# Six raw weight buffers for four, four common buffers fewer, and two steps moved in a block of a split-precision SwiGLU

## The chip, the cores and the metric

The kernel runs on one core of one Trainium2 chip. The metric is the device time in microseconds (us) of one execution; the median of several runs is compared. TensorE (PE) multiplies, VectorE (DVE) and ScalarE (ACT) work on its operands and results, GpSimd (POOL) does a few small things, and SyncE (SP) issues nearly all weight loads.

## The reference, cut to what matters

One decoder layer on 256 tokens of width 2048, in float32: a half-step SwiGLU FFN, a token mixer (sparse attention beside a recurrent branch), and a second FFN.

```python
D_MODEL, SEQ, D_FF = 2048, 256, 5632
def swiglu(h, w_in, w_out):
    a, b = jnp.split(h @ w_in, 2, axis=-1)
    return (jax.nn.silu(a) * b) @ w_out

h = layer_norm(DN_ALPHA * h + 0.5 * swiglu(h, ffn1_w_in, ffn1_w_out), ln1_g, ln1_b)
...
merged = g_attn * (y_attn @ w_attn_branch) + g_rnn * (y_rnn @ w_rnn_branch)
h = layer_norm(DN_ALPHA * h + merged @ w_out, ln2_g, ln2_b)
h = layer_norm(DN_ALPHA * h + 0.5 * swiglu(h, ffn2_w_in, ffn2_w_out), ln3_g, ln3_b)
```

## The kernel before

**Split operands.** Every float32 operand is kept as two parts, high (`wh`, `xs`/`hs`, `gh`) and low (`wl`, ..., `gl`), and a product is three matmuls: high x high, high x low, low x high (lines 734, 735, 736). A weight piece is 128 x 1024 numbers (512 KB). SP loads it (lines 192 and 206) into a raw buffer; ACT rounds it to `wh` (line 300); DVE subtracts that to get `wl` (line 301). High and low halves live in five buffers each (`HL_BUFS`), so piece n is split when piece n - 5 has been multiplied. `unit` asks for loads 8 pieces ahead and splits 4 ahead.

**Buffers.** `raw` tiles (4 KB a partition, `RAW_BUFS` = 4) hold loaded pieces. `u` tiles (2 KB a partition, `U_BUFS` = 53) are the common pool: activations in halves, sums of activations, residual, gate results, rows of gains and biases, attention's and the recurrent branch's tiles, and in the mixer the four quarters of a "quad" piece (loaded at line 204). Pieces P1 and Q5 of the FFN have buffers of their own (`k0`, four, and `k1`, three).

**An FFN** has 11 blocks of 512 hidden columns for gate and up. In blocks 1 to 10 most of the input product is done in Strassen's way with 7 products for 8: for each of three chunks (four k-tiles each) there are pieces P1, Q5, P6, Q3, P2, P7, Q4, each 6 matmuls, where some weights are sums of others, made by DVE in place (line 222): P6 needs P1 + Q5's quarter and the loaded P6 quarter, Q4 needs P1's buffer and the loaded P2 quarter. The fourth chunk is plain (`c`, four pieces of 12 matmuls). The output product of the block before is interleaved (`o`, 8 pieces of 12 matmuls).

**Banks and the join.** A block has four sums in PSUM: B and D in banks `bp`, A and E in the two banks `mm`. B starts with P1 and D with Q5. When P1 is complete, ACT writes A = -B (line 819 through `urgent`); P6 and then P7 add to A; after P7 ACT writes E = -A. D's first part is copied to `zd` when Q5 is complete, A's first part to `zu` when P6 is. The block's last plain piece completes all four; then comes the **join** (lines 853 to 863): silu of B and E on ACT, and on DVE zu += D, zu *= silu(B), zd += A, zd *= silu(E). Only zd += A reads bank A for the last time, so the next block's A can be written only after it. Both results are transposed on TensorE (line 1209) and split to `gh` and `gl` for the output product. An output pair of banks `ob` is copied out and the next pair seeded by ACT (lines 1238 and 1226).

**What sets the order.** PE, SP and POOL run in the order in which the code is written, which for an FFN is the plan of `wide_plan`: `STEADY` for blocks 2 to 9, `LAST` for block 10, a list of its own for block 1. In the strings, `o`, `c` and the form names are pieces in order, and `h` takes the next of the following block's head (P1, Q5, P1, Q5, P1, Q5), whose pieces stand among the present block's. ACT and DVE are ordered by a scheduler, which prefers what is marked urgent among what it holds for ready.

Of the kernel before, what the change touches and what calls it, by code (L numbers as in the profile page):

```python
# [12 lines left out]
OP = mybir.AluOpType  # L13
# [32 lines left out]
for _k, _w in (("ln1_g", NK), ("ln1_b", NK), ("ln2_g", NK), ("ln2_b", NK), ("ln3_g", 4), ("ln3_b", 4), ("conv_w", 4 * NR),  # L46
# [4 lines left out]

LAG = 2

U_BUFS = 53
T_BUFS = 8
RAW_BUFS = 4
K0_BUFS = 4
K1_BUFS = 3
HL_BUFS = 5
# [11 lines left out]
WGA, WAB, WRB, WO = (), (0, 1, 2, 3,), (0, 1, 2, 3,), (0, 1, 2,)  # L71


STEADY = ("o P6 o Q3 P6 Q3 o P6 o Q3 P2 o P7 o P7 P7 "
          "P2 P2 c Q4 o Q4 h c Q4 h o h c h h h c")
LAST = "o o P6 Q3 P6 Q3 o o P6 Q3 P2 P7 P7 P7 P2 P2 c Q4 Q4 c Q4 c c o o"


def wide_plan():

    def fast(n):
        return FAST[:2] if n == 1 else FAST

    def group(n, *items):
        return [(n, f, fast(n)[i]) for f, i in items if i < len(fast(n))]

    def head(n):  # L90
        return group(n, ("P1", 0), ("Q5", 0), ("P1", 1), ("Q5", 1), ("P1", 2), ("Q5", 2)) if n < NBK else []

    plan = [(0, "c", k) for k in range(NK)]
    for n in range(1, NBK):
        fill = [(n, "o", 0)]
        h = head(n + 1)
        plain = [(n, "c", k) for k in range(NK) if k // 4 not in fast(n)]
        if n == 1:
            plan += group(n, ("P1", 0), ("P1", 1), ("Q5", 0), ("Q5", 1), ("P6", 0), ("Q3", 0), ("P6", 1), ("Q3", 1))
            plan += 2 * fill + group(n, ("P2", 0)) + 2 * fill + group(n, ("P7", 0), ("P7", 1)) + 2 * fill  # L100
            plan += group(n, ("P2", 1))
            c0, c1, c2, c3 = (plain[i::4] for i in range(4))
            plan += c0 + group(n, ("Q4", 0), ("Q4", 1)) + h[:1] + c1 + h[1:3] + c2 + h[3:] + c3
            continue
        left = {}
        for f in (LAST if n == NBK - 1 else STEADY).split():
            i = left[f] = left.get(f, -1) + 1
            plan += fill if f == "o" else plain[i:i + 1] if f == "c" else h[i:i + 1] if f == "h" else group(n, (f, i))
    return plan


# [33 lines left out]
class Weights:  # L145
# [33 lines left out]
    def load_to(self, i):  # L179
        nc = self.nc  # L180
        while self.loaded <= min(i, len(self.pieces) - 1):
            ap, form = self.pieces[self.loaded]
            k = self.key(self.loaded)
            if isinstance(form, tuple):
                if form[0] in QUARTERS:
# [4 lines left out]
                    else:  # L190
                        t = self.pool.tile([P, PIECE], F32, name=f"raw{self.loaded}", tag="raw", bufs=RAW_BUFS)
                    nc.sync.dma_start(t, ap)
                    self.quarter[form[1], j] = t
            elif k not in self.raw:
# [5 lines left out]
                else:  # L200
                    t = self.pool.tile([P, PIECE], F32, name=f"raw{self.loaded}", tag="raw", bufs=RAW_BUFS)
                if form in QUADS.values():
# [52 lines left out]
    def small(self, name):  # L255
        return self.pool.tile([P, 512], F32, name=name, tag="u", bufs=U_BUFS)

# [119 lines left out]
def tile_layer(ctx, tc, x_fm, x_tm, pos, f1a, f1o, wA, wki, wB, wG, lru, lru_x, wab, wrb, wo, f2a, f2o,  # L377
# [5 lines left out]
    V, A, T, G = nc.vector, nc.scalar, nc.tensor, nc.gpsimd  # L383
    count = [0]

    def name(s):
        count[0] += 1
        return f"{s}{count[0]}"

    def U(s="u", dt=F32):  # L390
        return pool.tile([P, 512], dt, name=name(s), tag="u", bufs=U_BUFS)

# [28 lines left out]
    def BP():  # L421
        return psum.tile([P, 512], F32, name=name("bp"), tag="bp", bufs=4)
# [49 lines left out]
    for i in range(NR + LAG):  # L472
# [4 lines left out]
        if i >= LAG:  # L477
            g, c = divmod(i - LAG, TPG)
# [253 lines left out]
    def three(ps, xh, xl, w, start, stop, seeded=False):  # L732
        h, l = (v.rearrange("p (a h c) -> p a c h", h=2, c=P) for v in w)
        T.matmul(ps, xh, h, start=start, stop=False, skip_group_check=seeded)  # L734
        T.matmul(ps, xh, l, start=False, stop=False, skip_group_check=seeded)  # L735
        T.matmul(ps, xl, h, start=False, stop=stop, skip_group_check=seeded)  # L736

    def tokens(ps, x, t, w, start, stop, seeded=False):
        h, l = x(t) if callable(x) else (x[:, i, t * P:(t + 1) * P] for i in range(2))
        three(ps, h, l, w, start, stop, seeded)  # L740
# [67 lines left out]
    def xop(x, q, i, t):  # L808
        def op(r):
            v = x[4 * q + 2 * r + i]  # L810
            return v[:, 0, t * P:(t + 1) * P], v[:, 1, t * P:(t + 1) * P]
        return op

    def sop(forms, q, i):
        return lambda r: tuple(v[:, i * P:(i + 1) * P] for v in forms[2 * q + r])

    def urgent(f, *args, **kw):
        with tc.high_priority():
            f(*args, **kw)  # L819

    def blocksW(x, forms, fill, done):

        last = {(n, f): i for i, (n, f, k) in enumerate(PLAN)}
        bank = {n: {} for n in range(NBK)}
        z = {n: {} for n in range(NBK)}  # L830
        c = [None, None]

        def banks(t):
            if not c[t]:
                c[t] = [(CB, OB)[t]() for _ in range(2)]
            return c[t]

        def first(k, end):
            ws = [W.unit(512) for _ in range(2)]
            for t in range(2):  # L840
                for j in range(2):
                    tokens(banks(t)[j], x[k], t, ws[j], k == 0, k == NK - 1)
            for t in range(2 if end else 0):
                s = U("z")
                urgent(A.activation, s, c[t][0], AF.Silu)
                urgent(V.tensor_tensor, s, s, c[t][1], op=OP.mult)
                done(0, t, s)

        def plain(n, k, end):
            ws = [W.unit(512) for _ in range(2)]  # L850
            for t, j, b in ((0, 0, "B"), (0, 1, "D"), (1, 1, "A"), (1, 0, "E")):
                tokens(bank[n][b], x[k], t, ws[j], False, end, True)
            if end:
                v, ps = z[n], bank[n]
                s = [U("zs"), U("zs")]
                urgent(A.activation, s[0], ps["B"], AF.Silu)
                urgent(A.activation, s[1], ps["E"], AF.Silu)
                urgent(V.tensor_tensor, v["u"], ps["D"], v["u"], op=OP.add)
                urgent(V.tensor_tensor, v["u"], v["u"], s[0], op=OP.mult)
                done(n, 0, v["u"])  # L860
                urgent(V.tensor_tensor, v["d"], ps["A"], v["d"], op=OP.add)
                urgent(V.tensor_tensor, v["d"], v["d"], s[1], op=OP.mult)
                done(n, 1, v["d"])
                del bank[n], z[n]

        def product(n, form, k, end):
            b, op = {"P1": ("B", xop(x, k, 0, 0)), "P2": ("B", xop(x, k, 1, 0)), "Q3": ("D", sop(forms, k, 3)),
                     "Q4": ("E", xop(x, k, 1, 1)), "Q5": ("D", sop(forms, k, 0)), "P6": ("A", sop(forms, k, 1)),
                     "P7": ("A", sop(forms, k, 2))}[form]
            ps = bank[n]  # L870
            new = b not in ps
            if new:
                ps[b] = BP()
            for r in range(2):
                three(ps[b], *op(r), W.unit(512), new and r == 0, end and r == 1, form not in ("P1", "Q5"))
            if not end:
                return
            if form == "P1":
                ps["A"] = CB()
                urgent(A.activation, ps["A"], ps["B"], AF.Copy, scale=-1.0)  # L880
            elif form == "Q5":
                z[n]["d"] = U("zd")
                urgent(A.activation, z[n]["d"], ps["D"], AF.Copy)
            elif form == "P6":
                z[n]["u"] = U("zu")
                urgent(A.activation, z[n]["u"], ps["A"], AF.Copy)
            elif form == "P7":
                ps["E"] = CB()
                urgent(A.activation, ps["E"], ps["A"], AF.Copy, scale=-1.0)

        skip = 0
        if getattr(x, "halves", None):
            eager(x, banks)
            skip = 4
        for i, (n, form, k) in enumerate(PLAN):
            end = i == last[n, form]
            if i < skip:
                continue
            if form == "o":
                fill()  # L900
            elif n == 0:
                first(k, end)
            elif form == "c":
                plain(n, k, end)
            else:
                product(n, form, k, end)
# [384 lines left out]
    qT, kT, v, qiT = [None] * 8, [None] * 2, [None] * 2, [None] * 4  # L1291
# [182 lines left out]
    for b in a_order:  # L1474
# [9 lines left out]
        ps = blockA(hs)  # L1484
        if b == 5:
            for t in range(2):
                h, l = U("v", F32R), U("v", F32R)
# [13 lines left out]
    for nb in range(4):  # L1501
        if WGA and nb == WGA[0]:
            forms = make_forms(hs, QG)
        ps = column_block(hs, forms, MIXED["wG"].get(nb))
# [6 lines left out]
    for nb in range(4):  # L1511
        ps = column_block(ya, forms, MIXED["wab"].get(nb))
# [91 lines left out]
    for j in range(NR + LAG):  # L1604
# [5 lines left out]
        if j < NR:  # L1610
            ps = blockB(hs)
# [15 lines left out]
            ps = blockB(hs)  # L1627
# [3 lines left out]
        if j >= LAG:  # L1631
            i = j - LAG
            g, c = divmod(i, TPG)
# [5 lines left out]
            if c == TPG - 1:  # L1639
                ps = BP()  # L1640
# [31 lines left out]
    for nb in range(4):  # L1672
        if WO and nb == 3:
            mforms = make_forms(mg, U)
        ps = column_block(yr, forms, MIXED["wrb"].get(nb))
        for t in range(2):
            d = gr[nb][t]
# [115 lines left out]
```

## Time and profile before

| | us |
|---|---|
| median of 3 runs | 2253.88 |
| lowest and highest | 2251.0, 2257.98 |
| profiled execution | 2250.04 |
| its span (first to last instruction) | 2248.2 |

In the profile a row names the line, the engine, the operation and the tiles without their numbers, and ends with the idle time before it and what ended that. PEld is the weight load of TensorE, which runs beside the matmuls. Matmuls are pipelined and their ends are modelled: they overlap in the rows, so that a stall is seen from start to start. The first FFN lies between about 0 and 680 us, the mixer up to 1560, the second FFN behind it.

### The profile page before, as it was taken

How to read it: one execution, taken by the hardware profiler on the slowest of the kernel's cores; microseconds unless marked ns; L12 is line 12 of the kernel's file. 1: busy time of each engine (PE TensorE's matmuls, PEld its weight loads, DVE VectorE, ACT ScalarE, POOL GpSimd, SP SyncE). 2: the span in 40 equal slices, each digit the busy share in tenths (PEclk: the TensorE clock that was granted, in tenths of full speed). 3: DMA queues.
4: the chain of work that ended last, by engine and by line, in shares of the span. 5: the costliest groups of instructions: out<-in, count | busy, mean ns of one | idle time of the engine just before them, and what ended most of it. 6: DMA issues, size and time to landing. Idle time of an engine off the chain costs nothing.

```text
span 2248.2 us, 30930 instructions
## 1 busy us (share of the span) xinstructions
PE 2219.8 (99%) x11164; PEld 1939.3 (86%) x11164; DVE 1958.7 (87%) x2617; ACT 1559.6 (69%) x2222; POOL 22.4 (1%) x58
## 2 busy tenths in 40 slices
PE   9999999999999999999999999999999999999999
PEld 8888888888888888889999888898888888888887
DVE  7899999999988887678788886898999999999997
ACT  6777777777766556555688885555777777777774
POOL 0000000000001000000000000000000000000000
PEclk9999999999999999999999999999999999999999
DMA  8666655566666555566655566556666656665664
GB/s 302 215 225 218 205 192 203 197 204 215 211 206 219 175 182 164 161 214 199 209 177 188 184 203 235 194 194 195 215 220 210 219 199 223 220 209 193 206 213 157
DMA packets 133498, 459.33 MB, mean 204 GB/s; under 512 B 15040, under 2 KB 17856, under 8 KB 133344
## 3 DMA queue, kind: packets, MB, share of 16 engines
q1 hardware_dynamic: 130608, 449.37, 59.9%
q0 software_dynamic: 2160, 6.94, 1.0%
q8 instruction: 87, 1.43, 0.3%
q10 hardware_dynamic: 576, 1.05, 0.1%
q14 instruction: 67, 0.55, 0.1%
HBM read 455.20 MB, written 2.10 MB: 203 GB/s over the span
## 4 chain that ended last, share of the span: by engine, by line
PE 62%; DVE 17%; DMA 8%; issue 7%; ACT 5%; POOL 0%; ACTq 0%; SPq 0%; DVEq 0%; POOLq 0%
DVE wl L301 11%; PE ob L735 8%; PE ob L736 7%; PE ob L734 7%; PE mm L734 7%; PE mm L735 7%; PE mm L736 7%; DVE k L222 4%; DMA raw<-f2a 4%; DMA raw<-f1a 4%; PE bp L736 3%; PE bp L734 3%; PE bp L735 3%; ACT wh L300 3%; PE ob L723 2%
## 5 line engine op out<-in xcount | busy, mean ns | idle before, releaser
L301 DVE TENSOR_TENSOR wl<-raw,wh 128x1024 fp32r<-128x1024 f32 (+2 forms) x734 | 858.2, 1184 | 137.6 <-ACT wh L300 132.6
L300 ACT ACTIVATE wh<-raw 128x1024 fp32r<-128x1024 f32 (+2 forms) x734 | 741.4, 1025 | 320.0 <-PE mm L736 127.1
L301 DVE TENSOR_TENSOR wl<-k,wh 128x1024 fp32r<-128x1024 f32 x290 | 349.3, 1220 | 37.3 <-ACT wh L300 35.3
L300 ACT ACTIVATE wh<-k 128x1024 fp32r<-128x1024 f32 x290 | 302.7, 1056 | 112.4 <-DVE k L222 55.0
L735 PE MATMUL ob<-wl,gh 128*128 128x512 f32 x640 | 244.4, 382 | 9.8 <-DVE wl L301 9.8
L734 PE MATMUL ob<-wh,gh 128*128 128x512 f32 x640 | 244.6, 382 | 1.4 <-ACT ob L1226 1.4
L736 PE MATMUL ob<-wh,gl 128*128 128x512 f32 x640 | 242.7, 379 | 0.0
L222 DVE TENSOR_TENSOR k<-k,raw 128x1024 f32<-128x1024 f32 x174 | 211.6, 1219 | 32.0 <-DMA raw<-f1a 16.5
L734 PE MATMUL mm<-wh,hs 128*128 128x512 f32 x418 | 161.6, 387 | 0.0
L736 PE MATMUL mm<-wh,hs 128*128 128x512 f32 x418 | 158.5, 379 | 0.4 <-DVE hs L1054 0.4
L735 PE MATMUL mm<-wl,hs 128*128 128x512 f32 x418 | 158.5, 379 | 0.2 <-DVE wl L301 0.2
L735 PEld LDWEIGHTS ob<-wl,gh 128*128 128x128 f32 x640 | 121.0, 189 | 33.0 <-DVE wl L301 17.0
L734 PEld LDWEIGHTS ob<-wh,gh 128*128 128x128 f32 x640 | 121.0, 189 | 19.2 <-ACT ob L1226 2.8
L736 PEld LDWEIGHTS ob<-wh,gl 128*128 128x128 f32 x640 | 121.0, 189 | 17.1 <-DVE gl L819 0.5
L1238 ACT ACTIVATE y<-ob 128x512 f32<-128x512 f32 x152 | 89.5, 590 | 65.8 <-PE ob L736 65.7
L734 PE MATMUL ob<-wh,hs 128*128 128x512 f32 x304 | 118.4, 390 | 1.0 <-ACT hs L1053 1.0
L736 PE MATMUL ob<-wh,hs 128*128 128x512 f32 x304 | 115.5, 380 | 0.6 <-DVE hs L1054 0.6
L735 PE MATMUL ob<-wl,hs 128*128 128x512 f32 x304 | 115.2, 379 | 0.0
L723 PE MATMUL ob<-hs,wh 128*128 128x512 f32 x336 | 111.2, 382 | 0.0
L734 PE MATMUL bp<-wh,sh 128*128 128x512 f32 (+1 forms) x298 | 107.8, 362 | 1.3 <-ACT zd L819 1.3
L723 PE MATMUL mm<-hs,wh 128*128 128x512 f32 x320 | 106.7, 384 | 0.0
L735 PE MATMUL bp<-wl,sh 128*128 128x512 f32 (+1 forms) x298 | 106.1, 356 | 0.0
(404 smaller groups left out, 4828.2 us busy)
## 6 DMA issues: line engine op xcount, KB each, us to landing
raw<-f2a SPq DMA_DIRECT2D x118, 512.0 KB, 4.3
raw<-f1a SPq DMA_DIRECT2D x116, 512.0 KB, 4.5
raw<-f1o SPq DMA_DIRECT2D x88, 512.0 KB, 4.2
raw<-f2o SPq DMA_DIRECT2D x88, 512.0 KB, 3.7
raw<-wB SPq DMA_DIRECT2D x80, 512.0 KB, 4.5
raw<-wA SPq DMA_DIRECT2D x64, 512.0 KB, 3.5
raw<-wG SPq DMA_DIRECT2D x64, 512.0 KB, 3.6
k<-f1a SPq DMA_DIRECT2D x58, 512.0 KB, 6.9
```

The source lines that it names most:

```text
L222: self.nc.vector.tensor_tensor(v, v, self.quarter[q, j], op=OP.add)
L300: nc.scalar.activation(hp, src, AF.Copy)
L301: self.last = nc.vector.tensor_tensor(lp, src, hp, op=OP.subtract)
L723: T.matmul(ps, w[0], turns(x.rearrange("p a t -> p (a t)")), start=first, stop=False)
L734: T.matmul(ps, xh, h, start=start, stop=False, skip_group_check=seeded)
L735: T.matmul(ps, xh, l, start=False, stop=False, skip_group_check=seeded)
L736: T.matmul(ps, xl, h, start=False, stop=stop, skip_group_check=seeded)
L1238: A.activation(Y[t][nb], open_ps[t], AF.Copy, scale=0.5)
```

## The change

Four edits:

- `RAW_BUFS` goes from 4 to 6 and `U_BUFS` from 53 to 49: the same bytes, moved from the common pool to raw pieces, for the whole kernel.
- The last Q5 piece of the following block (the sixth of its head) no longer stands ahead of the block's last plain piece but behind the first output piece of the next block (`H`), in `STEADY`, `LAST` and the list of block 1.
- In the join the urgent instruction zd += A is written ahead of zu += D.

```diff
-U_BUFS = 53
+U_BUFS = 49
-RAW_BUFS = 4
+RAW_BUFS = 6
...
-STEADY = ("o P6 o Q3 P6 Q3 o P6 o Q3 P2 o P7 o P7 P7 "
-          "P2 P2 c Q4 o Q4 h c Q4 h o h c h h h c")
-LAST = "o o P6 Q3 P6 Q3 o o P6 Q3 P2 P7 P7 P7 P2 P2 c Q4 Q4 c Q4 c c o o"
+STEADY = ("o H P6 o Q3 P6 Q3 o P6 o Q3 P2 o P7 o P7 "
+          "P7 P2 P2 c Q4 o Q4 h c Q4 h o h c h h c")
+LAST = "o H o P6 Q3 P6 Q3 o o P6 Q3 P2 P7 P7 P7 P2 P2 c Q4 Q4 c Q4 c c o o"
...
-            plan += c0 + group(n, ("Q4", 0), ("Q4", 1)) + h[:1] + c1 + h[1:3] + c2 + h[3:] + c3
+            plan += c0 + group(n, ("Q4", 0), ("Q4", 1)) + h[:1] + c1 + h[1:3] + c2 + h[3:5] + c3
...
-            plan += fill if f == "o" else plain[i:i + 1] if f == "c" else h[i:i + 1] if f == "h" else group(n, (f, i))
+            plan += fill if f == "o" else plain[i:i + 1] if f == "c" else h[i:i + 1] if f == "h" else head(n)[5:] if f == "H" else group(n, (f, i))
...
+                urgent(V.tensor_tensor, v["d"], ps["A"], v["d"], op=OP.add)
                 urgent(V.tensor_tensor, v["u"], ps["D"], v["u"], op=OP.add)
                 urgent(V.tensor_tensor, v["u"], v["u"], s[0], op=OP.mult)
                 done(n, 0, v["u"])
-                urgent(V.tensor_tensor, v["d"], ps["A"], v["d"], op=OP.add)
                 urgent(V.tensor_tensor, v["d"], v["d"], s[1], op=OP.mult)
```

What this makes of the program is shown at the join of block 4, the one at 300 us in the trace. The first number in `wh149`, `raw153` or `k0_143` is the piece's place in the plan. Before, 147 is the last Q5, 148 the last plain piece, 149 the first output piece, 150 P6, 151 the second output piece; after, 147 is the plain piece, 148 the first output piece, 149 the last Q5, and from 150 on the numbers mean the same.

TensorE before, from the last matmul of the first output piece on:

```order
L736 MATMUL ob146_2610<-wh149_2644,gl136_2261 128x512
L734 MATMUL mm147_2664<-wh150_2654,sh28_367 128x512
L735 MATMUL mm147_2664<-wl150_2655,sh28_367 128x512
L736 MATMUL mm147_2664<-wh150_2654,sl29_368 128x512
L734 MATMUL mm147_2664<-wh150_2654,sh33_400 128x512
L735 MATMUL mm147_2664<-wl150_2655,sh33_400 128x512
L736 MATMUL mm147_2664<-wh150_2654,sl34_401 128x512
L1209 MATMUL bp151_2744<-ident_126,zu137_2319 128x128 x4
L734 MATMUL ob145_2609<-wh151_2668,gh130_2227 128x512
```

and after, from the same matmul:

```order
L736 MATMUL ob146_2609<-wh148_2625,gl134_2237 128x512
L734 MATMUL bp144_2575<-wh149_2644,sh69_775 128x512
L735 MATMUL bp144_2575<-wl149_2645,sh69_775 128x512
L736 MATMUL bp144_2575<-wh149_2644,sl70_776 128x512
L734 MATMUL bp144_2575<-wh149_2644,sh74_806 128x512
L735 MATMUL bp144_2575<-wl149_2645,sh74_806 128x512
L736 MATMUL bp144_2575<-wh149_2644,sl75_807 128x512
L1209 MATMUL bp151_2732<-ident_126,zu137_2319 128x128 x4
L734 MATMUL mm147_2664<-wh150_2654,sh28_367 128x512
```

The six matmuls of the last Q5 and the transposes of zu now stand between the output piece and P6, the first reader and writer of the new bank A (`mm147`).

VectorE before, around the four steps of the join (L819):

```order
L301 TENSOR_TENSOR wl150_2655<-k0_138_2420,wh150_2654 128x1024
L301 TENSOR_TENSOR wl151_2669<-raw151_2613,wh151_2668 128x1024
L222 TENSOR_TENSOR k0_143_2488<-k0_143_2488,raw153_2642 128x1024
L819 TENSOR_TENSOR zu137_2319<-bp122_2053,zu137_2319 128x512
L819 TENSOR_TENSOR zd126_2157<-mm125_2142,zd126_2157 128x512
L819 TENSOR_TENSOR zu137_2319<-zu137_2319,zs149_2700 128x512
L819 TENSOR_TENSOR zd126_2157<-zd126_2157,zs150_2701 128x512
L301 TENSOR_TENSOR wl152_2684<-raw150_2588,wh152_2683 128x1024
```

and after:

```order
L301 TENSOR_TENSOR wl150_2655<-k0_138_2420,wh150_2654 128x1024
L301 TENSOR_TENSOR wl151_2669<-raw151_2612,wh151_2668 128x1024
L819 TENSOR_TENSOR zu137_2319<-bp122_2053,zu137_2319 128x512
L819 TENSOR_TENSOR zd128_2202<-mm125_2142,zd128_2202 128x512
L819 TENSOR_TENSOR zu137_2319<-zu137_2319,zs148_2685 128x512
L819 TENSOR_TENSOR zd128_2202<-zd128_2202,zs149_2686 128x512
L301 TENSOR_TENSOR wl152_2696<-raw150_2588,wh152_2695 128x1024
```

The sum with `raw153` (for P6 of the second chunk) has left its place ahead of the join and stands some pieces earlier; the two first sums of the join stand as before, zu ahead of zd.

VectorE before, ahead of the eighth output piece (162):

```order
L301 TENSOR_TENSOR wl159_2816<-raw159_2738,wh159_2815 128x1024
L301 TENSOR_TENSOR wl160_2832<-raw160_2771,wh160_2831 128x1024
L222 TENSOR_TENSOR k0_138_2420<-k0_138_2420,raw159_2738 128x1024
L301 TENSOR_TENSOR wl161_2846<-k1_141_2457,wh161_2845 128x1024
L222 TENSOR_TENSOR k0_143_2488<-k0_143_2488,raw165_2843 128x1024
L222 TENSOR_TENSOR k0_146_2532<-k0_146_2532,raw166_2867 128x1024
L301 TENSOR_TENSOR wl162_2870<-raw162_2802,wh162_2869 128x1024
```

and after:

```order
L301 TENSOR_TENSOR wl159_2816<-raw159_2747,wh159_2815 128x1024
L222 TENSOR_TENSOR k0_138_2420<-k0_138_2420,raw159_2747 128x1024
L301 TENSOR_TENSOR wl160_2832<-raw160_2780,wh160_2831 128x1024
L222 TENSOR_TENSOR k0_143_2488<-k0_143_2488,raw165_2843 128x1024
L301 TENSOR_TENSOR wl161_2846<-k1_141_2457,wh161_2845 128x1024
L222 TENSOR_TENSOR k0_146_2532<-k0_146_2532,raw166_2867 128x1024
L301 TENSOR_TENSOR wl162_2870<-raw162_2802,wh162_2869 128x1024
```

The three sums that Q4 needs (with the loaded P2 quarters 159, 165 and 166) each move up by one split or stay; the `wl` of the output piece stands behind the last of them in both. The buffer that piece 166 is loaded into was, before, that of piece 160; after, it is that of piece 157.

## The prediction

> **What bounds the kernel now.** I read the page's busy line and its chain first, then the busy time by stage (windows), then what TensorE's weight loads waited for in each FFN, and last the timeline around one stall of each kind.
>
> ```profile
> span 2248.2 us, 30930 instructions
> ...
> PE 2219.8 (99%) x11164; PEld 1939.3 (86%) x11164; DVE 1958.7 (87%) x2617; ACT 1559.6 (69%) x2222; POOL 22.4 (1%) x58
> ...
> PE 62%; DVE 17%; DMA 8%; issue 7%; ACT 5%; POOL 0%; ACTq 0%; SPq 0%; DVEq 0%; POOLq 0%
> ...
> L300 ACT ACTIVATE wh<-k 128x1024 fp32r<-128x1024 f32 x290 | 302.7, 1056 | 112.4 <-DVE k L222 55.0
> ```
>
> TensorE is the bound: 28 us of the span without a matmul, and only 62% of the chain on it, the rest being work that it waited for. A weight piece is split by ACT (`wh`, 1.06 us) and then DVE (`wl`). The next view gives, for the first FFN, the mixer and the second FFN, the busy time of PE, PEld, DVE, ACT and POOL, the granted clock, DMA share and GB/s.
>
> ```profile
> 20.00:640.00 620.00, 610.62 (x2847) 528.82 (x2846) 569.84 (x548) 465.79 (x581) 0.00 (x0) 1.00 0.63 214
> 640.00:1560.00 920.00, 917.71 (x5083) 812.58 (x5082) 750.60 (x1399) 580.92 (x977) 8.74 (x15) 1.00 0.60 194
> 1560.00:2180.00 620.00, 610.00 (x2855) 527.22 (x2854) 576.59 (x592) 467.92 (x606) 9.27 (x16) 1.00 0.62 212
> ```
>
> The mixer has 2 us without a matmul in 920. Each FFN has about 10, and there VectorE is at 92% (569.84 of 620) and 93%. The clock is full everywhere, so a stall costs its length and no more. What the weight loads waited for, 100 to 640 us above the dots, 1640 to 2180 below (us, times, longest):
>
> ```profile
> PEld ob L735 <- DVE wl L301: 7.6, 9, 1.3
> PEld mm L734 <- ACT mm L819: 5.6, 7, 1.1
> ...
> PEld ob L735 <- DVE wl L301: 7.9, 9, 1.4
> PEld mm L734 <- ACT mm L819: 6.0, 8, 1.6
> ...
> PEld ob L736 <- DVE gl L819: 0.3, 1, 0.3
> ```
>
> Two stalls repeat about once a block. **Stall J** (join) is the first P6 piece, waiting until ACT has seeded bank A. **Stall O** is an output piece waiting for its low half `wl`. A gap's price is read at one of each; here J, in the block boundary at 300 us:
>
> ```profile
> 297.44 0.38 PE L734 MATMUL ob<-wh,gh 128*128 128x512 f32 x1
> 297.82 1.22 DVE L222 TENSOR_TENSOR k<-k,raw 128x1024 f32<-128x1024 f32 x1
> 298.96 0.68 DVE L819 TENSOR_TENSOR zu<-bp,zu 128x512 f32<-128x512 f32 x1
> 299.56 0.68 DVE L819 TENSOR_TENSOR zd<-mm,zd 128x512 f32<-128x512 f32 x1
> 299.60 0.38 PE L735 MATMUL ob<-wl,gh 128*128 128x512 f32 x1
> 299.82 0.38 PE L736 MATMUL ob<-wh,gl 128*128 128x512 f32 x1
> 300.10 0.58 ACT L819 ACTIVATE mm<-bp 128x512 f32<-128x512 f32 x1
> 300.74 0.48 PE L734 MATMUL mm<-wh,sh 128*128 128x512 f32 x1 [0.54 <-ACT mm L819]
> 301.06 0.38 PE L735 MATMUL mm<-wl,sh 128*128 128x512 f32 x1
> ...
> 302.13 0.60 PE L1209 MATMUL bp<-ident,zu 128*128 128x128 f32 x4
> 302.49 0.46 PE L734 MATMUL ob<-wh,gh 128*128 128x512 f32 x1
> ```
>
> Matmuls start 0.216 us apart (299.60 to 299.82) though each is drawn 0.38 long. From 299.82 to 301.06 two steps took 1.24 in place of 0.43: lost 0.81, where the weight loads of this stall stood idle 0.94. So a gap costs its row less 0.13. J: 11.6 - 15 x 0.13 = **9.6 us**. O: 15.5 - 18 x 0.13 = **13.2 us**. Together 22.8 us, 1% of the time; that is all these edits can reach directly.
>
> The chain of J: the last plain piece ends (297.44 starts the output piece behind it), DVE first finishes a sum of raw pieces, then zu, then zd, which alone frees bank A; ACT writes A; P6 starts. And O, at the eighth output piece of the same block:
>
> ```profile
> 316.29 0.33 SPq L192 DMA_DIRECT2D raw<-f1a  x1
> 320.90 1.23 DVE L222 TENSOR_TENSOR k<-k,raw 128x1024 f32<-128x1024 f32 x1 [1.23 <-DMA raw<-f1a]
> 322.04 1.22 DVE L301 TENSOR_TENSOR wl<-raw,wh 128x1024 fp32r<-128x1024 f32 x1
> 322.44 0.38 PE L734 MATMUL ob<-wh,gh 128*128 128x512 f32 x1
> 323.31 0.48 PE L735 MATMUL ob<-wl,gh 128*128 128x512 f32 x1 [0.50 <-DVE wl L301]
> ```
>
> DVE stood 1.23 us before the P2 sum whose raw piece was issued only at 316.29 (4.6 us to the sum's start), and the output's `wl` stands behind that sum. Over the whole run:
>
> ```profile
> DVE k L222 <- DMA raw<-f1a: 16.5, 19, 2.0
> ...
> DVE k L222 <- DMA raw<-f2a: 14.3, 18, 1.7
> ```
>
> That is about two such waits a block, 0.8 us each.
>
> **The change part by part.** No instruction is added or removed; pieces, waits and buffers move.
>
> *Last Q5 behind the first output piece.* PE now has 6 matmuls (6 x 0.216 = 1.30 us) between that piece and P6, and the four transposes of zu (0.36 us, 302.13 to 302.49) ahead of P6 too. P6 is wanted 2.59 + 1.30 + 0.36 = 4.25 us after the join in place of 2.59. The seed comes at the end of zd plus 0.54 + 0.58. DVE's row before zu is now a `wl` whose high-low buffer comes free when the last plain piece starts, 2.59 before the join; with both splits behind it (1.06 and the 1.22 of 322.04), zu starts at -0.3 at best, and at worst as now, at 1.5 (298.96 - 297.44). Zd starts 0.60 behind zu, so the seed ends between 1.4 and 3.2, and zu's product, which the transposes need at 3.9, ends between 1.6 and 3.4. J ends either way, with 0.5 us to spare at worst: **-9.6 us**. Late next could be Q3's bank, which waits for ACT's copy of the shifted Q5, now behind two splits on ACT; a P6 (1.30) and an output piece (2.59) cover it. Q5's DMA is issued two places later on SP, behind a plain and an output load, and is used two pieces later; POOL's order is the same.
>
> *Second half's sum first.* The order of DVE shows zu still ahead of zd at every join, since zu's bank is complete earlier. Worth 0; had it worked, the seed would come 0.60 us sooner (298.96 to 299.56), which J no longer needs.
>
> *Six raw buffers.* The raw piece of that P2 sum now takes the buffer of the output piece split five pieces before, whose `wl` ends by 312.85 in this trace, in place of 316.26:
>
> ```profile
> 311.64 4.62 DVE L301 TENSOR_TENSOR wl<-raw,wh 128x1024 fp32r<-128x1024 f32 x4
> ```
>
> (the first of four, 1.21 long). It is issued 3.4 us earlier and the wait of 1.23 goes. Does DVE then keep up? From the join to this `wl` it has 11 splits and 6 sums at 1.13 and six short steps at 0.60: 22.8 us, done 22.5 to 24.3 after the join. PE reaches that `wl` after five output pieces, nine short ones and two transposes: 12.95 + 11.7 + 0.7 + 0.2 = 25.6. So O goes with 1.3 us to spare; before, one more sum stood behind the join and one short piece less. In an FFN's last block four short pieces follow each other, and DVE there has no DMA wait to lose (busy 11.18 of 11.20 us in the first FFN):
>
> ```profile
> 601.00:612.20 11.20, 11.02 (x55) 9.31 (x54) 11.18 (x14) 9.73 (x15) 0.00 (x0) 1.00 0.36 121
> ```
>
> The same count gives 12.7 us of DVE there against 12.6 of PE, so I keep those two at O's mean, 2 x 13.2 / 18 = 1.5. O: **-11.7 us**.
>
> *Four common buffers fewer.* Quad loads of the mixer take them. Two of the rows of what SP waited for between 900 and 1060 us, in the branch with the first quads:
>
> ```profile
> SPq L206 <- DVE wl L301: 80.7, 31, 5.5
> ...
> SPq L204 <- PE ob L736: 1.0, 1, 1.0
> ```
>
> Quad loads (L204) waited about 1 us, raw loads 80.7, without PE losing anything in the mixer row above. Bounds: 0, or, if each of the 11 column blocks' quads held the queue as long as the longest raw wait (5.5) and nothing covered it, +60; I take 0, nearest to the L204 row. At the second FFN's start two row loads come later by the release of their buffers; the later one is first used here:
>
> ```profile
> 1609.55 0.54 POOL L694 DMA_DIRECT2D gr<-ln_g  x1 [21.42 <-DVE y L710]
> ...
> 1642.28 0.68 DVE L708 SCALAR_TENSOR_TENSOR y<-y,gr 128x512 f32<-128x512 f32 x1
> ```
>
> The 33 us between them cover a wait for the next buffer; 0.
>
> The sum: 9.6 + 11.7 = 21.3, less 1.3 for four or five new small waits of a reordered DVE, each like the 0.3 in the last row of the weight-load view: **-20 us**. The profiled execution took 2250.04 us; it would take 2230. The median shown is 3.84 above it, and the same saving gives 2253.88 - 20 = **2234 us**.
>
> **A rule against it.** DVE is busy more than the weight loads:
>
> ```profile
> 300.74:361.50 60.76, 59.69 (x279) 51.65 (x279) 55.77 (x52) 46.02 (x58) 0.00 (x0) 1.00 0.61 206
> ```
>
> Freed of its stalls (0.81 and O's mean, 0.73) a block is 59.2 us of PE against 55.8 drawn on DVE: DVE is the second bound, 3.4 us behind, and decides inside a block only. The Trainium skill (Perfetto Trace Analysis, Identifying the Most-Contended Engine) ranks by occupancy and takes TensorE by its weight loads; by it DVE comes first here, 87% to 86%, and a change that takes nothing off DVE should bring nothing at O, only J's 9.6. By this row's count it does not bound the block; the rule is the first rival.
>
> **Rivals.**
> 1. *DVE stays the limit at O.* For: VectorE's 92% in the FFN's row. Against: the 1.23 idle, and the 1.3 to spare. Only J goes: 2253.9 - 9.6 = 2244. The same time comes out if six transfers in flight each land later by what they start earlier (3.4 us); the DMA engines' share of 0.63 in the FFN's row speaks against. The Trainium skill (DMA: Bandwidth & Descriptors, Latency and other measured facts) puts memory latency at 0.2 us and at 2 us under high load; an estimate from that page is up to 1.8 us more, short of 3.4. No run here shows it.
> 2. *J stays in part*, the sums' order being unchanged: 13.2 alone goes, 2241. The 0.5 to spare at worst speaks against.
> 3. *ACT makes a new wait.* One split now stands before the second seed of the output banks:
>
> ```profile
> 306.84 0.60 ACT L1226 ACTIVATE ob<-y 128x512 f32<-128x512 f32 x1
> 307.75 1.06 ACT L300 ACTIVATE wh<-k 128x1024 fp32r<-128x1024 f32 x1 [0.30 <-DVE k L222]
> ...
> 309.49 0.38 PE L734 MATMUL ob<-wh,gh 128*128 128x512 f32 x1
> ```
>
> The seed ends at 307.44; the output piece starts at 309.49, so 2 us cover 1.06. If that split waits for its sum beyond the cover, about 1.06 a block comes back: 20 - 17 = 3 us saved, 2251, no change.
> 4. *Slower: quad loads hold SP's queue.* With 4 common buffers fewer a quad waits and all raw loads behind it starve PE. Eleven column blocks have a quad; the sign turns when each loses over 20/11 = 1.8 us beyond cover, and at 5.5 each, 60 - 20 = +40: 2294. Speaks against: L204's 1 us.
>
> **How the numbers follow.** Forecast 0.63; rival 1 0.15; 2 0.05; 3 0.10; 4 0.07. The forecast's own spread: all 22.8 and the second FFN's opening wait (1.5 us in its first block) gone, about 2227 with 2 us of run spread; half of O kept, 2240. The range reaches over rivals 1 and 2 to 2248 and leaves out most of 3 and all of 4. A measurement here tells about 0.3% (6.8 us) from no change. Faster by more: forecast, 1, 2: 0.83. Within: 0.11, mostly 3. Slower: 0.06.
>
> **What would show it.** In the profile after: the rows of PEld behind `ACT mm` gone or under 1 us an FFN; those behind `wl` under 2 us; DVE's waits for raw pieces of f1a and f2a under a third; PE steps from block to block near 59.2 us. The mixer's stretch stays at 920 us. I am wrong if DVE's idle time goes and PE's gaps stay (rival 1), if gaps at `ob` behind ACT appear (3), or if the mixer grows (4).

## The result

The changed kernel took **2225.06 us** (4 runs, 2224.74 to 2225.54), the kernel before 2253.23 (4 runs, 2251.0 to 2257.98). The ratio is 0.9872 with a 95% interval from 0.9855 to 0.989: faster by 28 us, 1.3%. Forecast were 2234 and a range from 2226: the direction is right, the time lies 0.9 us below the range, and the runs show that the path given for stall J, nearly half of the forecast gain, was wrong. The page of the changed kernel, with span, busy time and the shares of the chain of waits:

```profile
span 2223.0 us, 30937 instructions
...
PE 2210.0 (99%) x11164; PEld 1941.2 (87%) x11164; DVE 1953.3 (88%) x2617; ACT 1560.6 (70%) x2222; POOL 22.4 (1%) x58
...
PE 91%; DVE 3%; ACT 3%; issue 2%; DMA 1%; POOL 0%; ACTq 0%; DVEq 0%; POOLq 0%
```

The chain, which lay on TensorE for 62% before, lies on it for 91%. VectorE's busy time hardly changed (1958.7 to 1953.3): it does the same work, and TensorE no longer waits for it. The windows of the first FFN, the mixer and the second FFN (columns as in the prediction):

```profile
20.00:640.00 620.00, 619.32 (x2911) 541.56 (x2910) 577.28 (x575) 472.54 (x589) 0.00 (x0) 1.00 0.62 219
640.00:1560.00 920.00, 917.08 (x5081) 811.45 (x5080) 751.43 (x1403) 582.67 (x993) 12.63 (x21) 1.00 0.60 193
1560.00:2180.00 620.00, 618.18 (x2907) 540.28 (x2907) 583.27 (x579) 475.93 (x597) 5.37 (x10) 1.00 0.63 217
```

In a fixed stretch of 620 us TensorE now works 8.7 us more in the first FFN (610.62 before) and 8.2 more in the second; the mixer is as it was, 2 to 3 us without a matmul in 920. What the waits were, first between 20 and 100 us, then 100 to 640, then 1640 to 2180, and last VectorE's over the whole run:

```profile
PEld ob L734 <- ACT ob L1226: 1.1, 1, 1.1
PEld bp L734 <- ACT zd L819: 0.2, 1, 0.2
...
PEld ob L735 <- DVE wl L301: 0.3, 1, 0.3
...
PEld ob L735 <- DVE wl L301: 0.5, 1, 0.5
...
DVE k L222 <- DMA raw<-f2a: 1.9, 2, 1.7
DVE k L222 <- DMA raw<-f1a: 1.2, 3, 0.6
```

Stall J (`PEld mm L734 <- ACT mm`, 11.6 us before) is not in the list at all, stall O is down from 15.5 to 0.8, and VectorE's waits for raw pieces from 30.8 to 3.1. The join of block 4 in the timeline (the stretch that the prediction shows from 297 us on):

```profile
290.02 0.38 PE L734 MATMUL ob<-wh,gh 128*128 128x512 f32 x1
290.70 0.68 DVE L819 TENSOR_TENSOR zu<-bp,zu 128x512 f32<-128x512 f32 x1
290.71 1.05 ACT L300 ACTIVATE wh<-raw 128x1024 fp32r<-128x1024 f32 x1
...
291.30 0.68 DVE L819 TENSOR_TENSOR zd<-mm,zd 128x512 f32<-128x512 f32 x1
...
291.66 0.59 ACT L819 ACTIVATE mm<-bp 128x512 f32<-128x512 f32 x1
...
291.90 0.68 DVE L819 TENSOR_TENSOR zu<-zu,zs 128x512 f32<-128x512 f32 x1
...
293.90 0.60 PE L1209 MATMUL bp<-ident,zu 128*128 128x128 f32 x4
...
294.26 0.46 PE L734 MATMUL mm<-wh,sh 128*128 128x512 f32 x1
```

The join is at 290.02, where the output piece behind the last plain piece starts. Counted from there, P6 starts at 4.24 (forecast 4.25) and bank A is seeded by 2.23 (291.66 + 0.59; forecast 1.4 to 3.2): **2.0 us to spare**. The transposes of zu start at 3.88 (forecast 3.9), its product ends at 2.56 (forecast 1.6 to 3.4): only 1.3 to spare, which will matter below.

### The profile page after: what moved, and what is told of

Its sections match the earlier page's. It is cut to its first block, busy times and chain, and to the rows that moved or that the text cites. A ratio compares the mean times of both kernels' runs of the same rounds, so it can differ in the third digit from the quotient of the medians.

```text
span 2223.0 us, 30937 instructions
## 1 busy us (share of the span) xinstructions
PE 2210.0 (99%) x11164; PEld 1941.2 (87%) x11164; DVE 1953.3 (88%) x2617; ACT 1560.6 (70%) x2222; POOL 22.4 (1%) x58
## 3 DMA queue, kind: packets, MB, share of 16 engines
q10 hardware_dynamic: 576, 1.05, 0.1%
## 4 chain that ended last, share of the span: by engine, by line
PE 91%; DVE 3%; ACT 3%; issue 2%; DMA 1%; POOL 0%; ACTq 0%; DVEq 0%; POOLq 0%
PE ob L734 11%; PE ob L735 11%; PE ob L736 11%; PE mm L735 10%; PE mm L734 10%; PE mm L736 10%; PE bp L734 6%; PE bp L735 6%; PE bp L736 6%; PE ob L723 2%; PE mm L723 2%; DVE wl L301 2%; PE ob L724 1%; PE mm L724 1%; ACT wh L300 1%
## 5 line engine op out<-in xcount | busy, mean ns | idle before, releaser
L734 PE MATMUL ob<-wh,gh 128*128 128x512 f32 x640 | 244.7, 382 | 1.4 <-ACT ob L1226 1.4
L734 PE MATMUL mm<-wh,hs 128*128 128x512 f32 x418 | 161.6, 387 | 0.0
L734 PEld LDWEIGHTS ob<-wh,gh 128*128 128x128 f32 x640 | 121.0, 189 | 19.0 <-ACT ob L1226 2.5
L734 PE MATMUL ob<-wh,hs 128*128 128x512 f32 x304 | 118.4, 390 | 1.0 <-ACT hs L1053 1.0
L734 PE MATMUL bp<-wh,sh 128*128 128x512 f32 (+1 forms) x298 | 106.3, 357 | 0.0
```

## The experiments

All of them were run beside the kernel before, in three groups; its medians there were 2252.28, 2252.34 and 2251.7, and its 17 runs in the first group went from 2246.3 to 2255.21. A saving below is counted from the median of its own group.

| kernel | us | range | runs | ratio to before | 95% interval |
|---|---|---|---|---|---|
| six raw buffers only | 2225.17 | 2224.73 to 2226.47 | 4 | 0.9882 | 0.9869 to 0.9895 |
| moved Q5 piece only | 2233.7 | 2233.5 to 2234.8 | 5 | 0.992 | 0.9908 to 0.9932 |
| 49 common buffers only | 2253.54 | 2247.91 to 2261.49 | 12 | 1.0006 | 0.9995 to 1.0016 |
| changed, five raw buffers | 2225.34 | 2224.62 to 2226.15 | 4 | 0.9882 | 0.9869 to 0.9895 |
| six raw, old order at the join | 2228.98 | 2228.49 to 2231.94 | 4 | 0.9901 | 0.9887 to 0.9914 |
| four raw, new order at the join | 2229.16 | 2228.69 to 2230.56 | 4 | 0.99 | 0.9887 to 0.9913 |
| five raw buffers only | 2226.0 | 2225.91 to 2227.05 | 4 | 0.9885 | 0.987 to 0.99 |
| changed, 3.0 us of DVE a join | 2250.87 | 2249.55 to 2253.79 | 12 | 0.9999 | 0.999 to 1.0007 |
| changed, 1.2 us of DVE a join | 2227.2 | 2225.8 to 2228.25 | 4 | 0.9889 | 0.9876 to 0.9903 |
| changed, 1.2 us ahead of the sums | 2256.69 | 2254.87 to 2258.83 | 10 | 1.0025 | 1.0015 to 1.0034 |
| six raw, 1.2 us ahead of the sums | 2259.17 | 2257.79 to 2264.63 | 5 | 1.0035 | 1.0022 to 1.0049 |

**The parts alone.** First the parts of the change were taken apart. The edit that has no kernel of its own here is the one that writes the second half's sum first. In the trace above zu still goes ahead of zd (290.70, 291.30), as in the kernel before, and the next kernel, which lacks this edit, takes the same time as the changed one. The first kernel has only the buffers changed:

```diff
-U_BUFS = 53
+U_BUFS = 49
...
-RAW_BUFS = 4
+RAW_BUFS = 6
```

> Before with six raw buffers and 49 common buffers; the plans and the join as they were. Theory A (the two stalls are separate, as forecast): O goes and J stays, so 13 us below the kernel before, about 2240; weight loads behind ACT's seed of bank A keep about 11 us, those behind wl fall from 15.5 to under 3. Theory B (both stalls are one lateness of DVE between the join and the eighth output piece; there the changed kernel shows a wl done 1.8 us early, and without the moved piece one more sum of 1.13 stands ahead of it and TensorE comes 1.30 sooner): O is left at 0.4 to 0.6 a block and J as it was, so only 2 to 6 us below, about 2249. On the spread of the runs: if it comes from DVE's waits for transfers, all runs of this kernel lie within 1.5 us, since those waits fall from 31 to under 10 us; if it comes from the stalls themselves, they spread by 3 us or more like the kernel before.

Both theories fell. Six raw buffers alone save 27.1 us, all that the change saves; the moved piece adds nothing to them. The runs spread by 1.7 us. The timeline at the same join, of VectorE from the two sums on, then with ACT's split and seed and TensorE's P6:

```profile
284.92 2.35 DVE L222 TENSOR_TENSOR k<-k,raw 128x1024 f32<-128x1024 f32 x2
...
291.74 1.22 DVE L301 TENSOR_TENSOR wl<-raw,wh 128x1024 fp32r<-128x1024 f32 x1
292.87 0.68 DVE L819 TENSOR_TENSOR zu<-bp,zu 128x512 f32<-128x512 f32 x1
...
293.05 1.05 ACT L300 ACTIVATE wh<-k 128x1024 fp32r<-128x1024 f32 x1
...
293.47 0.68 DVE L819 TENSOR_TENSOR zd<-mm,zd 128x512 f32<-128x512 f32 x1
...
294.00 0.59 ACT L819 ACTIVATE mm<-bp 128x512 f32<-128x512 f32 x1
...
294.94 0.38 PE L734 MATMUL mm<-wh,sh 128*128 128x512 f32 x1
```

No sum stands between the last `wl` (291.74) and zu any more. The scheduler that orders VectorE has put the two sums with the second P6's raw piece into the time before the join (284.92), presumably because it reckons with that piece earlier. ACT's split of the first of these sums (293.05) has no idle time ahead of it, and the seed behind it ends 0.35 us before P6. So a number of buffers had changed the order of another engine's instructions.

The moved piece alone (the plan strings of the change, four raw and 53 common buffers):

> Before with the last Q5 piece behind the first output piece, four raw and 53 common buffers. Theory A: J goes and O stays, so 10 us below the kernel before, about 2243; weight loads behind wl keep 12 us or more. Theory B: this move alone frees DVE's stretch by 1.13 + 1.30 = 2.4 us a block, more than O's 0.73, so O goes too although DVE still waits for raw pieces: 20 us or more below, about 2232; rows behind wl under 4 us. On the spread: if it comes from transfers that reach TensorE through O, then it shrinks with O here too, under theory B.

It saves 18.6 us, more than J's 9.6, so it takes part of O with it. Theory B has the direction right; its saving of 20 us or more, with rows behind `wl` under 4 us, is too large. The waits:

```profile
DVE k L222 <- DMA raw<-f1a: 17.9, 26, 2.4
DVE k L222 <- DMA raw<-f2a: 11.3, 21, 1.7
PEld ob L735 <- DVE wl L301: 8.2, 15, 1.5
```

VectorE waits for raw pieces as long as before (29.2 us), but the rows behind `wl` are halved (17.0 before, over the whole run), which fits theory B's count of 2.4 us more for VectorE ahead of the eighth output piece.

Next the smaller common pool by itself:

```diff
-U_BUFS = 53
+U_BUFS = 49
```

> Before with 49 common buffers in place of 53 and nothing else. Forecast: 0, within 0.1% of the kernel before, the mixer's stretch 920 us. Rival (quad loads hold the queue): the mixer grows by 1.8 to 5.5 us for each of its 11 column blocks, 20 to 60 us slower.

No change, as forecast; the mixer's row is that of before:

```profile
640.00:1560.00 920.00, 917.71 (x5082) 812.38 (x5081) 751.44 (x1399) 581.35 (x977) 8.74 (x15) 1.00 0.62 194
```

Then a fifth raw buffer in place of the sixth, in the changed kernel:

```diff
-U_BUFS = 49
+U_BUFS = 51
...
-RAW_BUFS = 6
+RAW_BUFS = 5
```

> The changed kernel with five raw and 51 common buffers. Theory A (the raw buffers remove O): a fifth buffer lets the P2 piece start about half as early, so O comes back in part, 2 to 6 us slower than the changed kernel, 2227 to 2231. Theory B (the moved piece removes O): within 1.5 us of the changed kernel, 2225 to 2226.5, though DVE's waits for raw pieces are between 5 and 25 us.

With the moved piece, five are as good as six.

**Order or arrival.** Six buffers do two things: raw pieces arrive earlier, and VectorE's order changes. Next each was tried without the other. With six buffers, edges of issue order put the two sums back where they stood before, the first between the last `wl` and zu, the second behind the next chunk's `wl`; the join's rows are then the old ones:

```diff
...
+                with tc.issue_after(W.held.ins) if W.held else ExitStack():
+                    urgent(V.tensor_tensor, v["u"], ps["D"], v["u"], op=OP.add)
...
```

(and in `add` the same for each sum of the second P6's raw piece, behind the last `wl`).

> Six raw and 49 common buffers with the old plans, but DVE held to the old order at each join: the sum for the second P6 between the last wl and zu, the sum of its Q5 behind the wl of the second Q3. Theory C (what six buffers gave at the join is the order: they let that sum of 1.13 us move ahead of the join, so zd and the seed come 1.13 earlier than P6 needs): J is back at 9 to 10 us in all, and with two more sums in DVE's stretch O in part, 0 to 4 us; 2234 to 2240; rows of weight loads behind ACT's seed 10 to 16 us. Rival (the earlier arrival itself removed the stalls, whatever the order): J stays away and the time within 2 us of six raw buffers alone, 2225 to 2227.

The time is between the two, nearer the rival: 23.4 of the 27.1 us stay. The join of block 4, with VectorE, TensorE's first output piece, the seed and P6:

```profile
290.34 1.22 DVE L310 TENSOR_TENSOR wl<-raw,wh 128x1024 fp32r<-128x1024 f32 x1
...
291.48 1.22 DVE L226 TENSOR_TENSOR k<-k,raw 128x1024 f32<-128x1024 f32 x1
...
292.01 0.38 PE L744 MATMUL ob<-wh,gh 128*128 128x512 f32 x1
...
293.76 0.58 ACT L829 ACTIVATE mm<-bp 128x512 f32<-128x512 f32 x1
...
294.60 0.38 PE L744 MATMUL mm<-wh,sh 128*128 128x512 f32 x1
```

The sum is back between `wl` and zu, and there is still no stall: it starts 0.53 us *before* the join (291.48 against 292.01), where in the kernel before it started 0.38 *after* it (297.82 against 297.44). VectorE comes to the join 0.9 us earlier. What had held it before stands twelve microseconds ahead of the join, in the timeline of the kernel before (SP's queue, then VectorE):

```profile
280.61 0.33 SPq L192 DMA_DIRECT2D raw<-f1a  x1
...
285.24 1.23 DVE L222 TENSOR_TENSOR k<-k,raw 128x1024 f32<-128x1024 f32 x1 [0.82 <-DMA raw<-f1a]
...
289.79 1.22 DVE L222 TENSOR_TENSOR k<-k,k 128x1024 f32<-128x1024 f32 x1
292.14 1.22 DVE L301 TENSOR_TENSOR wl<-k,wh 128x1024 fp32r<-128x1024 f32 x1 [1.13 <-ACT wh L300]
```

The first sum adds the raw piece of the next block's first P6, issued at 280.61; VectorE stood 0.82 us for it. The delay goes on: the sum for the last Q5 is late (289.79), so is ACT's split of it, and so are the `wl` that waits for that (292.14) and the four behind it, up to the join.

How the late sum then reaches TensorE is not as the prediction has it, by way of zu and zd. ACT's rows at the same join of the kernel before, the split of this sum and the seed:

```profile
299.14 1.06 ACT L300 ACTIVATE wh<-k 128x1024 fp32r<-128x1024 f32 x1 [0.84 <-DVE k L222]
300.10 0.58 ACT L819 ACTIVATE mm<-bp 128x512 f32<-128x512 f32 x1
```

ACT stood idle 0.84 us for the sum of 297.82, split it, and wrote the seed next. The seed starts at 300.10, while zd += A is drawn to 300.24 (299.56 + 0.68), so it did not wait for zd. What is said further above, that the next A can be written only after zd += A, does not hold at this join. All 15 joins with stall J in the kernel before look like this: ahead of the seed stands a split for whose sum ACT was idle, by 0.14 to 1.52 us. The kernel with six buffers and the old order has two such joins left, the first of each FFN, and P6's weight load waited 1.1 and 2.4 us there. At both VectorE had stood for a raw piece just before. The later one:

```profile
1663.07 1.23 DVE L226 TENSOR_TENSOR k<-k,raw 128x1024 f32<-128x1024 f32 x1 [2.87 <-DMA raw<-f2a]
...
1666.66 1.06 ACT L309 ACTIVATE wh<-k 128x1024 fp32r<-128x1024 f32 x1 [2.40 <-DVE k L226]
1667.62 0.58 ACT L829 ACTIVATE mm<-bp 128x512 f32<-128x512 f32 x1
```

Then the other way round: four buffers, with the sums of the second P6 and the next `wl` held behind the join's four steps.

```diff
...
+                zd = urgent(V.tensor_tensor, v["d"], v["d"], s[1], op=OP.mult)
+                W.behind(W.last, zd)
+                if W.held:
+                    W.behind(W.held, zd)
...
```

> Four raw and 53 common buffers and the old plans; at each join DVE is held to zu, zd and their products first, and the two sums of the second P6's raw piece and the wl of the first Q3 behind them. Theory C (order): J goes, 9.6 us; the P2 sum before the eighth output piece falls behind that wl in this order too, so most of O's 13 goes as well: 2228 to 2234, although DVE's waits for raw pieces stay at 20 to 35 us. Rival (DVE is simply late in this stretch because raw pieces come late): what J gives comes back at O or at the P2 and P7 pieces behind it, and the time stays above 2240.

The order alone saves 23.2 us with four buffers. In block 4, the same wait for the first P6's piece, then zd, the seed and P6:

```profile
281.86 1.23 DVE L224 TENSOR_TENSOR k<-k,raw 128x1024 f32<-128x1024 f32 x1 [1.24 <-DMA raw<-f1a]
...
295.03 0.68 DVE L831 TENSOR_TENSOR zd<-mm,zd 128x512 f32<-128x512 f32 x1
...
295.75 0.58 ACT L831 ACTIVATE mm<-bp 128x512 f32<-128x512 f32 x1 [0.83 <-DVE zd L831]
...
296.39 0.47 PE L746 MATMUL mm<-wh,sh 128*128 128x512 f32 x1
```

VectorE waited 1.24 us for the raw piece, longer than before. The split of the second P6's sum no longer stands ahead of the seed, which now does wait for zd (its row says so; it starts 0.72 us after zd does, where before it was 0.54). It ends at 296.33, just in time for P6. So **J needed both**: VectorE's lateness, which begins with the wait of 0.8 at the first P6, and the late sum's split ahead of the seed on ACT. In block 4 either one taken away ends it. One thing was not as expected: over the whole run VectorE's waits for raw pieces fell too, to 5.4 and 3.7 us, so this run sets the order against the wait of block 4 and others like it, not against all of the waits.

Five raw buffers with the old plan:

> Old plans with five raw and 51 common buffers. Theory C (order): in the program the two sums of the second P6 already stand ahead of the join with five, so both stalls go as with six: 2225 to 2228. Rival (the start of each transfer counts): with a fifth buffer a P2 piece starts some 2 us earlier in place of 3.4, so a third or more of O's 13 us stays: 2229 to 2234.

Again nearly everything, 26.3 us, comes from one more buffer, and the rival (a third of O stays) falls.

**What bounds it now.** The Trainium skill (Perfetto Trace Analysis, Identifying the Most-Contended Engine) would still rank VectorE first, with 88% against 87% of the weight loads. So work was added to VectorE in the changed kernel:

```diff
                 urgent(V.tensor_tensor, v["d"], v["d"], s[1], op=OP.mult)
+                for _ in range(5):
+                    urgent(V.tensor_tensor, s[0], s[0], s[1], op=OP.add)
```

> The changed kernel with five more DVE adds of 128x512 (0.60 us each, 3.0 us) behind the products of each join, into a buffer that nothing reads afterwards; the output is the same. Theory T (TensorE bounds a block, DVE has 2.1 us idle behind the P2 pieces and the wl of the eighth output piece is done 1.8 us before its use): O comes back by 3.0 - 1.8 = 1.2 us in each of 20 joins, +24 us, 2249. Theory D (DVE is the bound, as its 88% busy against 87% of the weight loads says): the whole 3.0 us is added 20 times, +60 us, 2285.

It takes 25.8 us more than the changed kernel, 1.29 a join, as theory T said; theory D's 60 is out. The place was another than expected: the stall is at the third output piece of a block, not at the eighth (the `wl`, and the weight load that waits for it):

```profile
309.79 1.22 DVE L301 TENSOR_TENSOR wl<-raw,wh 128x1024 fp32r<-128x1024 f32 x1
...
311.05 0.19 PEld L735 LDWEIGHTS ob<-wl,gh 128*128 128x128 f32 x1 [1.72 <-DVE wl L301]
```

With two adds in place of five:

> The changed kernel with two more DVE adds (1.2 us) behind the products of each join, into a buffer that nothing reads. Theory T: 1.2 is under the 1.8 us by which the wl of the eighth output piece is early, so nothing comes back: 2225 to 2228. Theory D (DVE is the bound): 1.2 x 20 = +24, 2249.

It takes 2.1 us more where 24 were added, and the intervals of the two ratios overlap. So TensorE is the bound, and VectorE has between 1.2 and about 1.7 us (3.0 - 1.29) to spare behind a join.

**Is the moved piece a margin?** With six buffers it saves nothing. It might still be worth something where VectorE is later; so two adds were put ahead of the join's sums, in the changed kernel and in the one with six raw buffers alone.

```diff
...
+                for _ in range(2):
+                    r = urgent(V.tensor_tensor, U("zw"), ps["D"], v["u"], op=OP.add)
...
+                with tc.issue_after(r.ins):
+                    urgent(V.tensor_tensor, v["u"], ps["D"], v["u"], op=OP.add)
```

> The changed kernel with two more DVE adds (1.2 us) ahead of both sums of each join, unread; the wl issued last and the sums keep their place by an issue order. The move of the last Q5 piece is a margin at the join (there the seed now ends 2.0 us before P6 starts): 0 to 6 us over the changed kernel, 2225 to 2231. Rival (with six raw buffers the move buys nothing, as the run without it took the same time): the same loss here as in the next kernel, within 5 us.

> The same two adds (1.2 us) in the kernel with six raw buffers and the old plans, where the seed ends 0.35 us before P6 starts; the order also puts one sum of 1.13 ahead of zd. Margin theory: J is back with 0.9 to 2.0 us at each of some 18 joins, +16 to +36, 2241 to 2261, and weight loads behind ACT's seed read 16 us or more. Rival: within 5 us of the kernel before this one in the list.

The margin theory fell: 31.6 us more in the one, 34.0 in the other, the same within 5. The join of the changed kernel with the two adds, with TensorE's first output piece, the seed, zd's sum, the product of zu and the transposes:

```profile
294.00 0.38 PE L734 MATMUL ob<-wh,gh 128*128 128x512 f32 x1
...
295.65 0.59 ACT L819 ACTIVATE mm<-bp 128x512 f32<-128x512 f32 x1
...
297.01 0.69 DVE L819 TENSOR_TENSOR zd<-mm,zd 128x512 f32<-128x512 f32 x1
...
298.80 0.70 DVE L819 TENSOR_TENSOR zu<-zu,zs 128x512 f32<-128x512 f32 x1
...
299.64 0.41 PE L1215 MATMUL bp<-ident,zu 128*128 128x128 f32 x2 [1.59 <-ACT wh L300]
```

The loss is not at the seed but at the transposes of zu. Its product ends 5.50 us after the join (298.80 + 0.70 - 294.00), 2.56 without the adds. That is 2.94 later, more than the adds, because the scheduler also put two sums ahead of them (293.54 to 295.81). Less the 1.3 to spare, 1.6 us are lost, at 18 of the 20 joins: 29 of the 31.6. (The row names an ACT instruction. The nearest one ends at 299.63 (298.58 + 1.05), behind the start of the first weight load at 299.61; the product of zu ends 0.11 us before that start. In the other kernel the same rows name zu's product.)

The test did not reach the seed, though: it starts 1.36 us before zd += A here (295.65, 297.01), and 1.58 before it at the same join of the other kernel, so in neither does it stand behind what the adds delay. Whether the moved piece is a margin for the seed stays open. It is none for zu's product: the move puts six matmuls ahead of P6, but the transposes have stood behind one output piece and one short piece all along.

## Why the prediction was right and wrong

*TensorE is the bound, VectorE the second.* Right. A block takes 59.2 us now, as forecast, and the added work shows the room beside it.

*J, -9.6, by the moved piece.* J went, and the moved piece alone ends it too, but for one wait of 0.5 us. The **step failed in its path**: the prediction has the sum delay zu, then zd, and zd alone free bank A for the seed. In the kernel before the seed did not wait for zd; it stood on ACT behind the split of that sum, for which ACT was idle 0.84 us. The prediction's own rows show the seed starting (300.10) before zd has ended. Its 0.54 from zd's start to the seed's is a coincidence: both follow from the end of the sum, zd 0.60 behind it, and the seed 0.18 and the split's 0.96 behind it. At the join shown of the changed kernel the seed starts before zd has ended as well (291.66 against 291.98), behind a split of a loaded piece (290.71). So it came within the forecast bounds, 2.0 us early, partly by luck.

The step also stopped too soon. J goes as well with six or five buffers, which end VectorE's wait at the first P6, and with another order and four. That wait is its first half, and the prediction had the row for it: VectorE's waits for raw pieces were counted as "about two such waits a block, 0.8 us each", and only the one at O was used.

*O, -11.7, by six raw buffers.* It went, and with it J. **Adding the two failed**: the edits were added up as if each had a stall of its own, but alone they save 27.1 and 18.6 us, together 28. That the sum came out near the measurement is luck in this respect: the forecast gave each edit one stall, and six buffers end both.

*The terms of the sum.* The profiled executions took 2250.04 and 2224.74: 25.3 us in place of 20. The difference is in three terms, 4.9 us of the 5.3. O was kept in the last blocks (1.5), and went. New waits of a reordered VectorE (1.3) hardly came. And two waits in the first FFN's first block, which the prediction had not counted, shrank by about 2 (the kernel before, 20 to 100 us; after, 1.1 and 0.2):

```profile
PEld ob L734 <- ACT ob L1226: 1.8, 2, 1.4
PEld bp L734 <- ACT zd L819: 1.6, 1, 1.6
```

The wait at the second FFN's opening, which the range had allowed for, stayed.

*From the profiled execution to the median.* The median lies 8.8 us below the forecast: 5.3 come from the terms, 3.5 from this step, and either one alone would have left the time inside the range. The profiled execution of before lay 3.84 us under the median shown, and the forecast carried these 3.84 over to the changed kernel, whose profiled execution lies 0.3 us from its median. One execution of the kernel before can easily lie that far off: its runs spread by 8 to 9 us in each group, and those with 49 common buffers alone by 14 (12 runs). The other kernels of the table spread by 1 to 4 us (the last by 7), in 4 to 12 runs each. Why the kernels with J and O spread more stays open: the moved piece alone spreads by only 1.3 in five runs, although VectorE waits for transfers as long as before and half of O is left.

*The small terms.* Second half's sum first: 0, right as far as shown; zu still goes ahead of zd. Four common buffers fewer: 0, right.

*The rivals.* VectorE staying the limit at O, J staying in part, new waits of ACT and held quad loads did not come about. The one that matters most for the reasons was missing: that both stalls come from VectorE's lateness in the block, so that one edit alone does all.

## What to carry to other kernels

Compare the start of a stalled step with the end of the one that is thought to release it; if it starts earlier, look at what stands ahead of it on its own engine. Follow an engine's lateness back past its last instruction to the last time it stood idle: what it waited for there can be the cause, even if that lies ten microseconds and a dozen instructions ahead of the stall. Where several edits are made together, ask of each stall whether another edit would also end it, before gains are added. And a difference between the profiled execution and the median should not be carried over to a kernel that lacks the waits which may make it.

## What was not expected

One more raw buffer, 4 KB a partition, is enough here (2226.0 against 2225.2 with two more). Where a scheduler orders an engine, more buffers act twice: data come earlier, and the order changes with them; here each alone gives about 23 of the 27 us. And VectorE, 93% busy in the first FFN's stretch beside a TensorE that rests for 0.7 us in 620, had room for 1.2 us more in each block of 59.2 at a cost of 2 us in all.
